# GpSimd's elementwise work in mixer and output projection on VectorE, and x scaled by both factors in one operation

## The chip, the cores and the metric

The kernel runs on one core of one Trainium2 chip. A core has TensorE (matrix products), VectorE (DVE in the rows), ScalarE (ACT), GpSimd (POOL) and SyncE (SP), which here issues every transfer between memory and the on-chip pages. Each engine takes its instructions in the order in which they were written, and waits at the first whose inputs aren't there. The metric is the device time of one execution in microseconds. The kernel before took 2190.82 us, the median of three runs (2187.02 to 2191.81).

## The reference

One layer of a streaming encoder on x of 512 tokens by 2048 features, all in fp32. The elementwise steps that this change touches are the norms, the recurrent group and the gated residual:

```python
mod = silu(c) @ w_ada + b_ada                       # six vectors: sh1, sc1, gt1, sh2, sc2, gt2
h = modulate(rms_norm(x, g_mix), sh1, sc1)          # rms_norm(x)*(1 + sc1) + sh1
xr, yr, q, k, v, f_logit = split(h @ w_in)
# recurrent group, per 128 channels
u = causal_depthwise_conv(xr, conv_w, conv_b)
r, i = sigmoid(u @ w_a + b_a), sigmoid(u @ w_x + b_x)
log_a = -8 * r * softplus(-lam)
b_in = sqrt(-expm1(2 * log_a)) * (i * u)
y_rec = scan(exp(log_a), b_in) * gelu(yr)
# attention group: per-head norms of q and k, causal softmax with a forget bias
y_att = forgetting_attention(q, k, v, f_logit)
mix = concat(rms_norm(y_rec, g_out_rec), rms_norm(y_att, g_out_att))
x = x + gt1 * (mix @ w_out)
h2 = modulate(rms_norm(x, g_ffn), sh2, sc2)
gate, up = split(h2 @ w_up)
x = x + gt2 * ((silu(gate) * up) @ w_down)
```

## The kernel before, in words

Pages hold 128 features by 512 tokens. Every matrix product is made of three fp32r products: each operand is split into a high and a low part, the high part a rounded copy by ScalarE, the low part the difference by VectorE. These splits of the streamed weights are the *wsplits* (L187 ScalarE, L188 VectorE); TensorE waits for both halves. Low parts of activations are VectorE's too: `hpl` (L334), `hl` (L374).

The program is written stage by stage, and a scheduler fixes each engine's order when the program is built, by priorities and by its own estimates. Nothing is chosen at run time.

- *w1 stage* (about 5 to 109 us, loop `for kt in range(KT)`, L321). For each block of 128 features VectorE makes the row sums of `w_ada` times silu(c) for sc1 (two operations of 1024 columns, `ada` and `adf`, L149), forms the factor `A`, and the low parts of x·A and of the weights; ScalarE makes the high parts and the square of x; GpSimd adds the square to `ssq_x` (L280); TensorE multiplies for the recurrent input xr. The norm's factor comes last: after the sixteen blocks `rstd_x` is formed from `ssq_x` (`rms_rstd` on GpSimd, `rstd_parts`).
- *h stage* (109 to about 203 us). TensorE makes the first half of yr (`yr0p`) and head 0's q, k and v (`h0p`). `make_h` (L364) makes the normalised input: x·A was already made in place by ScalarE (L370, run in the w1 stage), GpSimd multiplies by `rstd_x` (L371), ScalarE adds `sh1` and rounds (`hh`, L373), VectorE makes `hl`. `ada_fast` makes sh1 from another two operations `ada` and `adf` a block, and `sh` (L366).
- *Heads* (203 to 606 us). For h = 1 to 7 TensorE runs a group `h1p` to `h7p` of 192 matmuls, and between them the attention of the head before (`stats`, `qk_t`, `score`, `pt_`, `pv`). VectorE evacuates each group: for head 0 also the forget logits `z` (L416) and the copies `qk` (L451). In the first two heads the 48 pieces of the projection's bias are summed: `bias_in` loads a piece `bw` (L566, two buffers) and VectorE adds it to `ba` (L569, L571); `bias_sum` gives them to TensorE as `binp` (L576). With the bias there, four pairs of recurrent blocks run beside heads 3 to 7 (`rec_pair`): `conv` reloads xr and multiplies by `rstd_x` (L588, GpSimd), `gates` multiplies i by u (L618, GpSimd), `scan` by the square root (L628, GpSimd) and scans (L630, VectorE), `finish` makes the gelu (`gelu2`, L543 on GpSimd) and the sum of squares.
- *Output projection* (606 to about 795 us). Four groups of 192 matmuls (`wo0p` to `wo3p`). For the first three ScalarE copies the result out of PSUM and GpSimd multiplies by `st_att[0]` (L803, L804); `x1_fin` then adds x and the squares to `ssq_1`.
- *FFN* (from 795 us on): up projection in seven products of halves (`uf`), down projection (`dn`). The change does not touch it.

## Time and profile before

| | |
|---|---|
| median of three runs | 2190.82 us (2187.02, 2190.82, 2191.81) |
| the profiled execution | 2185.2 us, its span 2183.5 us |
| TensorE (PE) busy | 2114.4 us, 97% of the span |
| VectorE (DVE) busy | 1560.4 us, 71%, 2319 instructions |
| ScalarE (ACT) busy | 873.1 us, 40% |
| GpSimd (POOL) busy | 187.3 us, 9%, 129 instructions |
| transfers | 406.01 MB, mean 186 GB/s |

Shares over the whole span hide the stages. In the page's forty slices of 54.6 us TensorE is at nine tenths or more from the 23rd slice to the last, while VectorE is at eight or nine tenths in the first four. GpSimd works in the first fourteen slices only. The rows below are therefore read for stretches of the span. Times in them are microseconds from the span's start; a row of a group of instructions gives its number, the busy time, the mean in nanoseconds of one, and the idle time just before it with what ended it.

### The profile page before, as it was taken

Reading aid. Unit: us, or ns where it says so; the run is one execution under the profiler, and the core shown is the slowest. Engines: PE = TensorE matmul, PEld = TensorE weight load, DVE = VectorE, ACT = ScalarE, POOL = GpSimd, SP = SyncE. Lnnn points to the kernel's source line nnn. Section 1 sums busy time; section 2 is a strip of 40 time slices with the busy share of each in tenths; the row PEclk is TensorE's granted clock in tenths of the full one; section 3 lists DMA queues with packets and bytes.
Section 4 is the critical chain, followed back from the end, with each engine's and each line's share of the span. In section 5 each row is a group of like instructions: output and inputs, shape, how many; then the busy total and the mean of one; then the engine's idle time right before and its main releaser. Section 6 shows DMA issues by size and latency. Waiting matters only on the chain.

```text
span 2183.5 us, 32375 instructions
## 1 busy us (share of the span) xinstructions
PE 2114.4 (97%) x12737; PEld 1911.2 (88%) x12737; DVE 1560.4 (71%) x2319; ACT 873.1 (40%) x1224; POOL 187.3 (9%) x129
## 2 busy tenths in 40 slices
PE   8988989899989999999999999999999999999999
PEld 6777988788878888899999999999999888888887
DVE  8998668886687879988888888888888343322332
ACT  5523436665343335544444444444444222221111
POOL 2260012332012400000000000000000000000000
PEclk9999989999999999999999999999999999999999
DMA  9868666566667752343434444343444984553442
GB/s 320 319 209 301 220 217 212 197 211 236 215 228 259 252 193 97 129 133 126 145 118 131 139 131 131 126 141 121 128 143 149 338 312 174 189 197 134 155 156 103
DMA packets 133017, 406.01 MB, mean 186 GB/s; under 512 B 14561, under 2 KB 19841, under 8 KB 123138
## 3 DMA queue, kind: packets, MB, share of 16 engines
q1 hardware_dynamic: 132866, 403.96, 54.6%
q8 instruction: 99, 1.62, 0.3%
q14 instruction: 52, 0.43, 0.1%
HBM read 361.15 MB, written 42.75 MB: 185 GB/s over the span
## 4 chain that ended last, share of the span: by engine, by line
PE 77%; DVE 12%; DMA 6%; issue 3%; ACT 2%; POOL 1%; SPq 0%; DVEq 0%; POOLq 0%; ACTq 0%
PE dn_0p L192 5%; PE dn_3p L192 5%; PE dn_2p L192 5%; PE dn_1p L192 5%; PE up0p L192 2%; PE wo3p L192 2%; PE wo2p L192 2%; PE wo1p L192 2%; DVE adf L149 2%; PE wo0p L192 2%; DMA ada<-in_adaT 2%; PE yr1p L192 1%; PE h3p L192 1%; DMA bw<-in_wyr 1%; DVE ada L149 1%
## 5 line engine op out<-in xcount | busy, mean ns | idle before, releaser
L139 DVE SCALAR_TENSOR_TENSOR ada<-ada,c_b 128x1024 f32<-128x1024 f32 x128 | 163.7, 1296 | 34.1 <-DMA ada<-in_adaT 33.9
L188 DVE TENSOR_TENSOR uq_0tl<-uq_0r,uq_0th 128x1024 fp32r<-128x1024 f32 x40 | 49.0, 1225 | 61.8 <-ACT uq_0th L187 61.7
L187 ACT ACTIVATE uq_0sh<-uq_0r 128x1024 fp32r<-128x1024 f32 x40 | 42.5, 1062 | 90.6 <-PE uf33p L957 2.3
L188 DVE TENSOR_TENSOR uq_0al<-uq_0r,uq_0ah 128x1024 fp32r<-128x1024 f32 x40 | 49.0, 1225 | 39.1 <-ACT uq_0ah L187 39.1
L187 ACT ACTIVATE uq_1th<-uq_1ra 128x1024 fp32r<-128x1024 f32 x40 | 42.5, 1062 | 70.6 <-DVE uq_1sl L188 1.8
L187 ACT ACTIVATE uq_0th<-uq_0r 128x1024 fp32r<-128x1024 f32 x40 | 42.4, 1060 | 70.6 <-DVE uq_0r L937 1.9
L187 ACT ACTIVATE uq_1sh<-uq_1rb 128x1024 fp32r<-128x1024 f32 x40 | 42.5, 1062 | 70.3 <-PE uf43p L957 2.4
L187 ACT ACTIVATE uq_1ah<-uq_1ra 128x1024 fp32r<-128x1024 f32 x40 | 42.5, 1062 | 60.6 <-issue 59.1
L187 ACT ACTIVATE uq_0ah<-uq_0r 128x1024 fp32r<-128x1024 f32 x40 | 42.4, 1060 | 49.3 <-issue 46.8
L149 DVE SCALAR_TENSOR_TENSOR adf<-adf,c_b 128x1024 f32<-128x1024 f32 x32 | 56.4, 1763 | 1.7 <-DMA adf<-in_adaT 1.7
L188 DVE TENSOR_TENSOR uq_1tl<-uq_1ra,uq_1th 128x1024 fp32r<-128x1024 f32 x40 | 49.0, 1226 | 10.3 <-ACT uq_1th L187 10.2
L192 PE MATMUL w1p<-hph,w1h 128*128 128x512 f32 x128 | 48.7, 407 | 6.4 <-ACT hph L333 6.1
L192 PE MATMUL w1p<-hpl,w1h 128*128 128x512 f32 x128 | 51.8, 405 | 2.0 <-DVE hpl L334 1.9
L188 DVE TENSOR_TENSOR uq_0sl<-uq_0r,uq_0sh 128x1024 fp32r<-128x1024 f32 x40 | 49.1, 1226 | 3.6
L571 DVE SCALAR_TENSOR_TENSOR ba<-bw,sh,ba 128x512 f32<-128x512 f32 x45 | 34.2, 769 | 23.8 <-DMA bw<-in_w 12.5
L188 DVE TENSOR_TENSOR uq_1sl<-uq_1rb,uq_1sh 128x1024 fp32r<-128x1024 f32 x40 | 49.0, 1226 | 2.7 <-ACT uq_1sh L187 0.6
L192 PE MATMUL w1p<-hph,w1l 128*128 128x512 f32 x128 | 50.7, 396 | 0.0
L188 DVE TENSOR_TENSOR uq_1al<-uq_1ra,uq_1ah 128x1024 fp32r<-128x1024 f32 x40 | 48.7, 1216 | 0.1
L149 DVE SCALAR_TENSOR_TENSOR ada<-ada,c_b 128x1024 f32<-128x1024 f32 x32 | 41.2, 1288 | 2.6 <-DMA ada<-in_adaT 2.6
L188 DVE TENSOR_TENSOR dn_1l<-dn_2r,dn_1h 128x1024 fp32r<-128x1024 f32 x11 | 13.5, 1226 | 38.0 <-ACT dn_1h L187 38.0
L188 DVE TENSOR_TENSOR dn_0l<-dn_2r,dn_0h 128x1024 fp32r<-128x1024 f32 x11 | 13.5, 1225 | 37.6 <-ACT dn_0h L187 37.6
L188 DVE TENSOR_TENSOR dn_1l<-dn_0r,dn_1h 128x1024 fp32r<-128x1024 f32 x11 | 13.5, 1225 | 37.4 <-ACT dn_1h L187 37.4
(13791 smaller groups left out, 8322.5 us busy)
## 6 DMA issues: line engine op xcount, KB each, us to landing
ada<-in_adaT SPq DMA_DIRECT2D x160, 512.0 KB, 5.0
uq_0r<-in_wups SPq DMA_DIRECT2D x80, 512.0 KB, 4.2
uq_1ra<-in_wups SPq DMA_DIRECT2D x40, 512.0 KB, 4.0
uq_1rb<-in_wups SPq DMA_DIRECT2D x40, 512.0 KB, 3.2
adf<-in_adaT SPq DMA_DIRECT2D x32, 512.0 KB, 5.4
actd<-ach SPq DMA_DIRECT2D x44, 256.0 KB, 2.0
actd<-acl SPq DMA_DIRECT2D x44, 256.0 KB, 4.1
dn_0r<-in_wdown SPq DMA_DIRECT2D x11, 1024.0 KB, 4.9
```

The costliest lines, as they stand in the source:

```text
L139: nc.vector.scalar_tensor_tensor(out=t, in0=t, scalar=1.0, in1=cs, op0=ALU.mult, op1=ALU.mult, accum_out=ac)
L149: nc.vector.scalar_tensor_tensor(out=t, in0=t, scalar=1.0, in1=c_b[:, cs], op0=ALU.mult, op1=ALU.mult, accum_out=ada_acc[j][:, hf, i:i + 1])
L187: nc.scalar.activation(R(hi[:, :n]), raw_ap, AF.Copy)
L188: tail_lo.append(nc.vector.tensor_sub(R(lo[:, :n]), raw_ap, hi[:, :n]).ins)
L192: nc.tensor.matmul(ps, lhsT=R(l), rhs=R(r), start=start, stop=stop)
L571: nc.vector.scalar_tensor_tensor(out=ba[j], in0=src, scalar=s1, in1=ba[j], op0=ALU.mult, op1=ALU.add)
```

## The change

Nine places are edited. In the w1 stage, in attention, in the recurrent blocks and behind the output projection the sums of squares go from GpSimd to VectorE (`square_acc`). In `make_h` ScalarE's product by `A` and GpSimd's by `rstd_x` become one VectorE operation with both factors, which stands where the h stage needs it. The products of xr by `rstd_x`, of i by u and by the square root go to VectorE. Gelu's square goes from GpSimd to ScalarE. The result of the output projection is multiplied by `st_att[0]` by VectorE straight out of PSUM, without ScalarE's copy. GpSimd keeps the small operations of `rms_rstd` and the constants.

```diff
--- before.py
+++ after.py
@@ -271,13 +271,13 @@
         sums()
         return spread()
 
-    def square_acc(ssq, src, first, name, tag, eng=None):
+    def square_acc(ssq, src, first, name, tag):
         if first:
             nc.scalar.activation(ssq, src, AF.Square)
         else:
             sq = page(name, tag)
             nc.scalar.activation(sq, src, AF.Square)
-            (eng or nc.gpsimd).tensor_add(ssq, ssq, sq)
+            nc.vector.tensor_add(ssq, ssq, sq)
 
     def log1p_exp(dst, z, w, name):
         e = small(w, name + "e", 2)
@@ -367,8 +367,7 @@
                                        in1=vcol(V_BADA + SH1 * KT, kt), op0=ALU.add, op1=ALU.add)
         sh1.append(s1)
         t = xs[kt]
-        nc.scalar.activation(t, t, AF.Copy, scale=A[kt])
-        nc.gpsimd.tensor_mul(t, t, rstd_x)
+        nc.vector.scalar_tensor_tensor(out=t, in0=t, scalar=A[kt], in1=rstd_x, op0=ALU.mult, op1=ALU.mult)
         h, l = page(f"hh{kt}", "h"), page(f"hl{kt}", "h")
         nc.scalar.activation(R(h), t, AF.Identity, bias=s1)
         nc.vector.scalar_tensor_tensor(out=R(l), in0=t, scalar=s1, in1=h, op0=ALU.add, op1=ALU.subtract)
@@ -540,7 +539,7 @@
     hs = [None] * NB
     def gelu2(y, name, tag):
         w = page(name, tag)
-        nc.gpsimd.tensor_mul(w, y, y)
+        nc.scalar.activation(w, y, AF.Square)
         nc.vector.scalar_tensor_tensor(out=w, in0=w, scalar=1.0 / GELU_C, in1=y, op0=ALU.add, op1=ALU.mult)
         nc.scalar.activation(w, w, AF.Tanh, scale=GELU_C * GELU_S)
         nc.vector.scalar_tensor_tensor(out=w, in0=w, scalar=1.0, in1=y, op0=ALU.add, op1=ALU.mult)
@@ -585,7 +584,7 @@
             x = page(f"xrl{n}", "c")
             nc.sync.dma_start(out=x, in_=xr[n])
             X[n] = x
-            nc.gpsimd.tensor_mul(x, x, rstd_x)
+            nc.vector.tensor_mul(x, x, rstd_x)
             nc.scalar.activation(x, x, AF.Identity, bias=bin_[:, n:n + 1])
             u = page(f"u{n}", "c")
             nc.scalar.activation(u, x, AF.Identity, scale=vcol(V_CW, n * 4 + 3), bias=vcol(V_CB, n))
@@ -615,7 +614,7 @@
                 for n in ns:
                     last["exp"] = nc.scalar.activation(RG[n], RG[n], AF.Exp, scale=spn[:, n:n + 1])
             for n in ns:
-                nc.gpsimd.tensor_mul(IG[n], IG[n], U[n])
+                nc.vector.tensor_mul(IG[n], IG[n], U[n])
             for n in ns:
                 nc.vector.tensor_mul(U[n], RG[n], RG[n])
                 nc.vector.scalar_tensor_tensor(out=X[n], in0=U[n], scalar=1.0, in1=X[n], op0=ALU.add, op1=ALU.mult)
@@ -625,7 +624,7 @@
                 for n in ns:
                     nc.scalar.activation(X[n], X[n], AF.Sqrt, scale=-1.0)
             for n in ns:
-                nc.gpsimd.tensor_mul(IG[n], IG[n], X[n])
+                nc.vector.tensor_mul(IG[n], IG[n], X[n])
             for n in ns:
                 nc.vector.tensor_tensor_scan(out=U[n], data0=RG[n], data1=IG[n], initial=0.0, op0=ALU.mult, op1=ALU.add)
                 hs[n] = U[n]
@@ -651,7 +650,7 @@
     def rec_out(n, g):
         y = hs[n]
         nc.vector.scalar_tensor_tensor(out=y, in0=g, scalar=0.5, in1=y, op0=ALU.mult, op1=ALU.mult)
-        square_acc(ssq_rec, y, n == 0, f"sqr{n}", "c", nc.vector if n >= 4 else nc.gpsimd)
+        square_acc(ssq_rec, y, n == 0, f"sqr{n}", "c")
         if n < 4:
             hs[n] = drp.tile([P, S], F32, name=f"yrecd{n}")
             nc.sync.dma_start(out=hs[n], in_=y)
@@ -800,8 +799,7 @@
             t = page(f"x1_{kt}", "c")
             gt = mods[GT1][:, kt:kt + 1]
             if g < 3:
-                nc.scalar.activation(t, ps[f], AF.Copy)
-                nc.gpsimd.tensor_mul(t, t, st_att[0])
+                nc.vector.tensor_mul(t, ps[f], st_att[0])
             else:
                 xt = load_x(kt, "x3_")
                 nc.vector.scalar_tensor_tensor(out=t, in0=ps[f], scalar=gt, in1=st_att[0], op0=ALU.mult, op1=ALU.mult)
@@ -810,7 +808,7 @@
             if g < 3:
                 late.append(lambda t=t, kt=kt: x1_fin(t, kt))
             else:
-                square_acc(ssq_1, t, kt == 0, f"sq1_{kt}", "d", nc.vector)
+                square_acc(ssq_1, t, kt == 0, f"sq1_{kt}", "d")
             if g == 3:
                 with_a2()
             if g == 3 and f == 0:
```

The scheduler builds new orders from this. On VectorE in a block of the w1 stage (`adf`: the second product with `w_ada`; `A`: the factor; `w1l`: a weight's low part), the difference of the two orders:

```order
 L149 SCALAR_TENSOR_TENSOR adf_3_293,ada_acc_114<-adf_3_293,c_b 128x1024
 L328 SCALAR_TENSOR_TENSOR A_302<-ada_acc_114,bg 128x1
+L280 TENSOR_TENSOR ssq_x<-ssq_x,sqx_315 128x512
 L330 TENSOR_TENSOR A_302<-A_302,vec 128x1
 L341 TENSOR_TENSOR w1l_310<-w1r_0_298,w1h_309 128x512
```

The sum of squares stands between the two steps of `A`, in every block from the second on.

On VectorE at the end of the h stage, around the last `hl` and up to the first `z` of head 0 (`ba`: the sums of bias pieces `bw`; `h_0l`, `h_1l`: wsplits), before:

```order
L569 TENSOR_SCALAR ba_1810<-bw_1_1815,sh_0_1042 128x512
L569 TENSOR_SCALAR ba_1811<-bw_2_1818,sh_0_1042 128x512
L188 TENSOR_TENSOR h_1l<-h0r_1678,h_1h 128x784
L374 SCALAR_TENSOR_TENSOR hl_1663<-x_920,sh_15_1658,hh_1662 128x512
L571 SCALAR_TENSOR_TENSOR ba_1809<-bw_0_1849,sh_1_1068,ba_1809 128x512
L188 TENSOR_TENSOR h_0l<-h1r_1791,h_0h 128x768
L571 SCALAR_TENSOR_TENSOR ba_1810<-bw_1_1852,sh_1_1068,ba_1810 128x512
L571 SCALAR_TENSOR_TENSOR ba_1811<-bw_2_1855,sh_1_1068,ba_1811 128x512
L188 TENSOR_TENSOR h_1l<-h1r_1791,h_1h 128x768
L571 SCALAR_TENSOR_TENSOR ba_1809<-bw_0_1929,sh_2_1110,ba_1809 128x512
L416 TENSOR_TENSOR z<-h0p_1416,bfb 128x8
```

and in the same place now:

```order
L370 SCALAR_TENSOR_TENSOR x_920<-x_920,A_926,rstd_x 128x512
L188 TENSOR_TENSOR h_1l<-h1r_1775,h_1h 128x768
L366 SCALAR_TENSOR_TENSOR sh_15_1643<-ada_acc_113,vec 128x1
L568 TENSOR_SCALAR ba_1793<-bw_0_1796,sh_0_1042 128x512
L568 TENSOR_SCALAR ba_1794<-bw_1_1799,sh_0_1042 128x512
L373 SCALAR_TENSOR_TENSOR hl_1647<-x_920,sh_15_1643,hh_1646 128x512
L450 COPY qk_1720<-h0p_1407 128x256
L415 TENSOR_TENSOR z<-h0p_1406,bfb 128x8
```

Before, there are seven `ba` operations ahead of `z`, one above these rows and six in them. Now there are two; the others have gone behind `z`. The new last scaling of x (L370) stands in front of the last `sh`. The transfers of the two remaining pieces now stand beside those of blocks 6 and 7 of sh1.

On TensorE in head 2's stretch (`h3p`: the group of head 3; `binp`: the bias sums), the first `binp` with its neighbours before:

```order
L192 MATMUL h3p_2677<-h_0h,hl_1073 128x384
L192 MATMUL h3p_2678<-h_0h,hh_1072 128x384
L192 MATMUL h3p_2678<-h_0l,hh_1072 128x384
L192 MATMUL h3p_2678<-h_0h,hl_1073 128x384
L576 MATMUL binp<-ones,ba_1809 128x1 x4
L192 MATMUL h3p_2675<-h_1h,hh_1114 128x384
```

and now:

```order
L192 MATMUL h3p_2662<-h_0l,hh_1226 128x384
L192 MATMUL h3p_2662<-h_0h,hl_1227 128x384
L192 MATMUL h3p_2659<-h_1h,hh_1251 128x384
L192 MATMUL h3p_2659<-h_1l,hh_1251 128x384
L575 MATMUL binp<-ones,ba_1793 128x1 x4
L192 MATMUL h3p_2659<-h_1h,hl_1252 128x384
```

Before, 24 matmuls of h3 stand ahead of the first `binp`, now 74; what is ahead of h3 is the same. The matmuls of attention and gates keep their places.

## Rows read from the trace of the kernel before

**Rows 1.** Stretches: PE, PEld, DVE, ACT, POOL busy; PEclk, DMA share, GB/s.

```profile
20.00:104.00 84.00, 80.97 (x336) 61.30 (x335) 80.82 (x129) 43.15 (x71) 20.97 (x14) 1.00 0.93 327
...
117.00:149.00 32.00, 29.47 (x130) 24.07 (x129) 29.54 (x24) 7.58 (x10) 31.34 (x16) 1.00 0.47 163
149.00:200.00 51.00, 44.75 (x223) 40.81 (x222) 46.15 (x82) 16.50 (x22) 0.00 (x0) 0.97 0.84 286
...
314.00:555.00 241.00, 221.30 (x1143) 201.29 (x1144) 187.42 (x305) 147.27 (x258) 63.01 (x42) 0.95 0.63 211
...
664.00:840.00 176.00, 176.00 (x788) 146.06 (x787) 138.69 (x170) 66.47 (x89) 40.25 (x24) 1.00 0.65 221
```

**Rows 2.** Waits of PE over the span: us in total, times, longest.

```profile
PE s L495 <- DVE nm L499: 10.3, 4, 3.1
PE pt L509 <- DVE bt L503: 8.2, 5, 2.4
...
PE h1p L192 <- DVE z L416: 5.9, 1, 5.9
...
PE binp L576 <- DVE ba L571: 1.3, 1, 1.3
```

**Rows 3.** Timeline, one block of the w1 stage: start us, us, engine, line.

```profile
44.09 1.22 DVE L149 SCALAR_TENSOR_TENSOR ada<-ada,c_b 128x1024 f32<-128x1024 f32 x1
...
45.00 1.47 POOL L280 TENSOR_TENSOR ssq_x<-ssq_x,sqx 128x512 f32<-128x512 f32 x1 [4.51 <-ACT sqx L279]
...
45.23 2.31 DVE L149 SCALAR_TENSOR_TENSOR adf<-adf,c_b 128x1024 f32<-128x1024 f32 x1
...
49.46 0.69 DVE L341 TENSOR_TENSOR w1l<-w1r,w1h 128x512 fp32r<-128x512 f32 x1
...
50.07 1.22 DVE L149 SCALAR_TENSOR_TENSOR ada<-ada,c_b 128x1024 f32<-128x1024 f32 x1
```

**Rows 4.** Groups of instructions of DVE in 20:104.

```profile
L149 DVE SCALAR_TENSOR_TENSOR adf<-adf,c_b 128x1024 f32<-128x1024 f32 x14 | 31.2, 2229 | 0.0
```

**Rows 5.** Chain that ended last, in order of time: start us, us.

```profile
209.05 6.66 PE h1p L192 x24
...
229.35 4.17 PE h1p L192 x24
...
663.84 43.52 PE wo1p L192 x192
```

**Rows 6.** Timeline of POOL in 95:170.

```profile
117.34 31.34 POOL L371 TENSOR_TENSOR x<-x,rstd_x 128x512 f32<-128x512 f32 x16 [1.93 <-ACT rstd_x L265]
```

**Rows 7.** Groups of instructions of DVE in 117:150.

```profile
L149 DVE SCALAR_TENSOR_TENSOR adf<-adf,c_b 128x1024 f32<-128x1024 f32 x4 | 8.1, 2034 | 0.0
L374 DVE SCALAR_TENSOR_TENSOR hl<-x,sh,hh 128x512 fp32r<-128x512 f32 x5 | 8.1, 1621 | 3.5 <-ACT hh L373 3.5
L149 DVE SCALAR_TENSOR_TENSOR ada<-ada,c_b 128x1024 f32<-128x1024 f32 x4 | 7.0, 1761 | 0.0
L366 DVE SCALAR_TENSOR_TENSOR sh<-ada_acc,vec 128x1 f32<-128x1 f32 x3 | 3.6, 1190 | 0.0
```

**Rows 8.** Timeline of DVE: the last hl, the first z, the last ba.

```profile
198.59 0.74 DVE L374 SCALAR_TENSOR_TENSOR hl<-x,sh,hh 128x512 fp32r<-128x512 f32 x1
...
208.84 0.16 DVE L416 TENSOR_TENSOR z<-h0p,bfb 128x8 f32<-128x8 f32 x1
...
310.55 1.41 DVE L571 SCALAR_TENSOR_TENSOR ba<-bw,sh,ba 128x512 f32<-128x512 f32 x2
```

**Rows 9.** Groups of instructions of DVE in 314:606.

```profile
L468 DVE TENSOR_TENSOR qk<-qk,ss 128x512 f32<-128x512 f32 x10 | 14.1, 1445 | 9.1 <-POOL ss L241 9.1
```

**Rows 10.** One line's instructions: ns min/median/max, first and last start.

```profile
L630 DVE TENSOR_TENSOR_SCAN u<-g,g x8: 1192/2268/2303, 368.4 to 524.8; 128x512 f32<-128x512 f32 x8
```

**Rows 11.** Groups of instructions of POOL over the span.

```profile
L588 POOL TENSOR_TENSOR xrl<-xrl,rstd_x 128x512 f32<-128x512 f32 x8 | 13.8, 1728 | 29.8 <-DMA xrl<-xrd 28.8 <-issue 0.9
...
L628 POOL TENSOR_TENSOR g<-g,xrl 128x512 f32<-128x512 f32 x8 | 12.2, 1550 | 21.8 <-ACT xrl L626 21.8
```

## The prediction

> **What bounds the kernel now.** I read the table of stretches first [rows 1]. In 664–840 us TensorE is busy all the time, and the page shows the same for nearly everything behind it, so whatever the change does there is hidden. The gaps lie in the first 664 us: 3.0 us in 20–104, 2.5 in 117–149, 6.3 in 149–200, 19.7 in 314–555. Up to 200 us VectorE is the fullest engine (80.8 of 84, 29.5 of 32, 46.2 of 51 us), while the transfers take 0.93, 0.47 and 0.84 of their engines' time. TensorE's own waits [rows 2] name VectorE most: the scores and the transposes of the weights in attention, and one wait of 5.9 us for `z`. So the question is whether VectorE, which receives 88 more operations of 512 columns, becomes fuller or emptier.
>
> **Term 1, the w1 stage (20–104 us).** One block of 128 rows shows it [rows 3]. GpSimd's sum starts at 45.00 and holds until 46.47. The `adf` product that VectorE starts at 45.23 takes 2.31 us, its twin `ada` of the same shape 1.22: it ends 1.1 us after GpSimd does. This is no accident of one block: all fourteen `adf` here average 2229 ns [rows 4]. So each GpSimd sum costs VectorE 1.09 us. On VectorE the sum costs 0.61 (a `w1l` of its shape starts at 49.46, the next instruction at 50.07). Net −0.48 of a block that lasts 5.98 us (`ada` at 44.09 and 50.07); 14 blocks, −6.7. Two floors lie close. TensorE needs 24 matmuls of 0.227 us (192 in 43.52 [rows 5]), 5.44 a block, which would allow −7.5. The transfers at full share would take 0.93 of 5.98, 5.56, which allows −5.9. Since all three then lie within 0.15 us of each other, I take −5.5, bounds −1 (transfers slow down near their limit) and −7.
>
> The Trainium skill's page "Perfetto Trace Analysis", section "Optimizing Scalar/DVE Operations", points the other way: where VectorE is saturated, hand work to ScalarE or even GpSimd; it adds that the two share a read port, so that it might not help. By the advice alone this stage would become 14 x 0.61 = 8.5 us longer; by its second sentence, and by [rows 3], it becomes shorter. The skill's page "SBUF — State Buffer", section "Who interferes with whom", calls that port pair an exclusive lock, on which the second to start waits for the whole of the first; the end of this `adf`, 1.1 us behind GpSimd's, agrees.
>
> **Term 2, the h stage (104–200 us).** GpSimd does all sixteen products x·rstd in one piece, 31.3 us from 117.34 on [rows 6]. VectorE's operations in that time are long [rows 7]: four `adf` at 2.03 and four `ada` at 1.76 for 1.22, five `hl` at 1.62 for 0.74 [rows 8], three `sh` of one column at 1.19, for which I count 0.22: 3.3 + 2.2 + 4.4 + 2.9 = 12.8 us of blocking, and by the same 1.09 two more wsplits, some 15 in all. After the change VectorE scales x itself, sixteen operations with two page operands and one column scalar. That is the form of `hl`: 0.74 us, less the 0.08 by which an instruction here overlaps the next (`w1l` lasts 0.69, the next starts after 0.61), 0.66; bounds 0.61 and 0.74. 16 x 0.66 = 10.6: net −4.4. At the stage's head some 0.7 more goes, since a GpSimd product stood between `rstd_x` and the first `hh`, and VectorE's short waits for transfers late in the stage should shrink, as its demand is now even. Against that the spills of xr move into this stage, and TensorE comes within 2 us of being the bound. I take −5, bounds 0 and −9.
>
> **Term 3, the hand-over to head 0 (200–209 us).** The last `hl` ends at 199.33, but the evacuation `z` runs only at 208.84 [rows 8]: VectorE, which takes instructions in order, stands before `ba` sums whose weights are still in transfer. TensorE waits 5.9 us for it [rows 2], and its first 24 matmuls after that take 6.66 us, against 4.17 for 24 later ones [rows 5]. In the new order (shown with the change) seven `ba` operations ahead of `z` have become two, with weights that were asked for some thirty transfers earlier. So `z` should follow the last `hl` by some 3 us instead of 9.5: −6.5, and up to −2.5 from the slow matmuls. I take −8, bounds −4 and −9.
>
> **Term 4, what is late next.** Those five operations aren't gone. After `z`, 46 `ba` operations with a load each remain in place of 41. Before, 41 took from 208.84 to 311.96 [rows 8], 2.5 us each, through two buffers. TensorE's `binp` needs the last of them and waited 1.3 us for it [rows 2], so the two paths were even. In the new order the first `binp` stands 50 matmuls of h3 later, 8.7 us at 0.174 (24 in 4.17 [rows 5]). TensorE now reaches it 8.7 − 1.3 − 2.5 (the slow matmuls) = 4.9 us later after `z` than before, other waits unchanged. Five more loads at 2.5 us are 12.5 us: a wait of some 8, up to 12 where the other waits shorten. With two buffers the loads can also go faster (two of 3.6 us at a time are 1.8 each), and then nothing waits. I take +5, bounds 0 and +12.
>
> **Term 5, the recurrent pairs (314–606 us).** 32 products and sums move: 32 x 0.61 = 19.5 us more on VectorE. What it gets back stands in its long operations: 10 `qk` at 1445 ns [rows 9] for the 0.69 of a `w1l`, 7.6 us; 8 scans, half of them over 2268 ns where the shortest took 1192 [rows 10], some 6; smaller ones I put at 8. Its waits for GpSimd's products before the scans go as well, and partly become waits for ScalarE's roots. So VectorE is about as full as before or some us emptier, and each product ends 0.7 to 1 us sooner. TensorE's waits for VectorE in the attention are 18.5 us [rows 2]; I let a quarter go: −4, bounds −12 and +9 (both below). Gelu's square goes to ScalarE, four times 0.6 us (estimate, by VectorE's 0.61), on an engine that is idle for 94 of 241 us [rows 1].
>
> **Term 6, output projection.** Twelve products go from GpSimd, behind a ScalarE copy, to one VectorE operation out of PSUM, and eleven sums of squares follow. TensorE has no gap in 664–840; its cover is VectorE's 37 idle us there (176 − 138.7 [rows 1]), while 23 x 0.61 = 14 come on. 0; without cover at most +14, which I don't count.
>
> Sum: −5.5 − 5 − 8 + 5 − 4 = −17.5 us. The profiled execution took 2185.2 us (span 2183.5 and 1.7 around it), so 2167.7; the median of the timed runs is 5.6 above it, 2190.8. Against that median I predict 2173 us, with 2164 to 2183 as its own range: the bounds of the terms seldom fall on one side together.
>
> **Rivals.**
> *More.* If TensorE's waits in attention are mostly the work of blocked VectorE operations, term 5 is −12, and with term 4 at 0 the sum is −30.5: 2160. For it: the two long groups of waits [rows 2] are for VectorE. Against: VectorE's queue there stays nearly as long as it was.
> *The transfers bind.* The first stage stands at 0.93 already [rows 1]. If that is the ceiling, terms 1 and 2 shrink to −1 each, and the loads of term 4, closer together, cost +8; with −8 and −2 the sum is −4: 2187. Against: 117–149 ran at 0.47, so there is room to bring loads forward.
> *Slower: waits at the head of VectorE's queue.* GpSimd stood idle 28.8 us for the reloads of xr and 21.8 for ScalarE's roots [rows 11] with nobody behind it; on VectorE the wsplits that feed TensorE stand behind these products. If half of the 50 us lands there and half of that reaches TensorE, term 5 is −4 + 13 = +9; with term 3 at −4 and term 4 at +12 the sum is +6.5: 2197. It decides from some 20 us of new VectorE idle time on. Against: much of this idle time is GpSimd being early, and the new order puts the products behind other work.
> *Slower: a full VectorE only gets fuller.* Were no blocking given back, terms 1 and 2 would be +8.5 and +10.6; with −8 and +5, +16: 2207. [Rows 3 and 7] speak against it. This is what the advice of "Perfetto Trace Analysis" in the Trainium skill would lead one to expect.
>
> **How the numbers follow.** Forecast 0.62, more 0.16, transfers 0.11, queue 0.08, fuller 0.03. A difference below 0.2% (4.4 us) can't be told from none here. Slower: the last two, less 0.01 for a mild queue, 0.10. Same: half of the transfers' case and 0.02 of the forecast's tail, 0.08. Faster: the rest, 0.82. The range for eight in ten runs from the larger gain, 2160, to just past the transfers' case, 2188.
>
> **What would show it.** Term 1: `adf` at 1.22 us throughout, a block of 5.4 to 5.6 us. Term 2: no `hl` above 0.8 us, the last `hl` 8 to 13 us before 199.3. Term 3: no wait of TensorE for `z` above 2 us, h1's first matmul near 190. Term 4: a wait before `binp` of some 5 us. Term 5: scans at 1.2 us, less of TensorE's time lost before scores, no VectorE idle time above 3 us before the products with xr. Behind 915 us all is shifted and nothing else. I am wrong if a block stays near 6 us, or if h4 to h7 take longer than before.

## The result and the profile after

The changed kernel takes 2161.57 us (median of four runs, 2160.31 to 2162.5), the kernel before beside it 2191.32 (four runs, 2187.02 to 2192.39): ratio 0.9868, 95% interval 0.9852 to 0.9883, or 29 us less. The forecast was 2173 with a range of 2160 to 2188, so the sign was right and the time lies near the range's lower end, outside the likeliest case's own 2164 to 2183. The profiled execution took 2160.95 us (before: 2185.2). The profiles are thus 24 us apart where the medians are 30: the profiled run of the kernel before is one of its faster ones, and leads over its profile come out some 5 us small by the end of the span.

First the same stretches as in [rows 1], the columns are as there:

```profile
20.00:104.00 84.00, 84.00 (x376) 69.35 (x374) 80.30 (x158) 37.76 (x63) 0.00 (x0) 1.00 0.96 350
117.00:149.00 32.00, 32.00 (x143) 26.50 (x142) 32.00 (x55) 10.19 (x14) 0.00 (x0) 1.00 0.92 315
149.00:200.00 51.00, 49.26 (x277) 48.31 (x275) 46.49 (x93) 17.45 (x29) 1.84 (x2) 1.00 0.88 303
314.00:555.00 241.00, 221.09 (x1158) 197.58 (x1157) 187.21 (x340) 150.93 (x265) 13.77 (x10) 0.98 0.65 218
664.00:840.00 176.00, 176.00 (x790) 146.12 (x789) 135.31 (x201) 66.62 (x88) 2.17 (x2) 1.00 0.58 198
```

In 20–104 us TensorE has no gap left and does 376 matmuls where it did 336; VectorE, as full as before, does 158 operations for 129. The transfers go at 350 GB/s, so 327 was not their ceiling. TensorE's waits over the span, which answer to [rows 2]:

```profile
PE pt L508 <- DVE bt L502: 14.3, 8, 4.0
PE s L494 <- DVE nm L498: 10.5, 5, 3.1
...
PE binp L575 <- DVE ba L570: 3.8, 1, 3.8
...
PE pc L422 <- DVE lf L420: 3.0, 1, 3.0
...
PE h3p L192 <- ACT v L453: 2.5, 1, 2.5
```

The wait for `z` is gone, that for `binp` has grown from 1.3, that of `pc` for `lf` from 0.2; `h3p` waited for `v` before too (3.1). The two of attention are longer in sum than before (24.8 us for 18.5). One block of the w1 stage, VectorE, in order of time, answers to [rows 3]:

```profile
43.02 1.22 DVE L149 SCALAR_TENSOR_TENSOR adf<-adf,c_b 128x1024 f32<-128x1024 f32 x1
...
44.42 0.69 DVE L280 TENSOR_TENSOR ssq_x<-ssq_x,sqx 128x512 f32<-128x512 f32 x1
...
48.38 1.22 DVE L149 SCALAR_TENSOR_TENSOR adf<-adf,c_b 128x1024 f32<-128x1024 f32 x1
```

A block lasts 5.36 us (43.02 to 48.38), and `adf` is short. Groups of VectorE in 101–185 us, the h stage (for [rows 7]):

```profile
L149 DVE SCALAR_TENSOR_TENSOR adf<-adf,c_b 128x1024 f32<-128x1024 f32 x15 | 18.2, 1215 | 0.0
L370 DVE SCALAR_TENSOR_TENSOR x<-x,A,rstd_x 128x512 f32<-128x512 f32 x16 | 11.9, 744 | 2.8 <-ACT rstd_x L265 2.8
L373 DVE SCALAR_TENSOR_TENSOR hl<-x,sh,hh 128x512 fp32r<-128x512 f32 x16 | 11.9, 744 | 0.0
```

The scaling costs 0.744 us each, as `hl` does, and nothing is held up. The last `hl` and the first `z` (for [rows 8]), and the bias sums over the span with their idle time:

```profile
182.05 0.75 DVE L373 SCALAR_TENSOR_TENSOR hl<-x,sh,hh 128x512 fp32r<-128x512 f32 x1
...
184.04 0.17 DVE L415 TENSOR_TENSOR z<-h0p,bfb 128x8 f32<-128x8 f32 x1
```

```profile
L570 DVE SCALAR_TENSOR_TENSOR ba<-bw,sh,ba 128x512 f32<-128x512 f32 x45 | 33.3, 749 | 27.7 <-DMA bw<-in_w 14.7 <-DMA bw<-in_wyr 13.0
```

Before, the last of these rows was

```profile
L571 DVE SCALAR_TENSOR_TENSOR ba<-bw,sh,ba 128x512 f32<-128x512 f32 x45 | 34.2, 769 | 23.8 <-DMA bw<-in_w 12.5 <-DMA bw<-in_wyr 11.1
```

`z` follows the last `hl` by 1.2 us where it followed by 9.5. VectorE waits 27.7 us for bias weights; it waited 23.8 us for them before, so the wait itself is hardly new, only its place is. Groups of VectorE in 314–606 us, for [rows 9 to 11]:

```profile
L629 DVE TENSOR_TENSOR_SCAN u<-g,g 128x512 f32<-128x512 f32 x8 | 9.5, 1213 | 0.0
L467 DVE TENSOR_TENSOR qk<-qk,ss 128x512 f32<-128x512 f32 x10 | 6.5, 688 | 9.0 <-POOL ss L241 9.0
L627 DVE TENSOR_TENSOR g<-g,xrl 128x512 f32<-128x512 f32 x8 | 5.5, 686 | 0.3
...
L587 DVE TENSOR_TENSOR xrl<-xrl,rstd_x 128x512 f32<-128x512 f32 x7 | 4.8, 688 | 4.8 <-DMA xrl<-xrd 4.8
```

Every operation is now about as short as the shortest of its kind before (1192 ns for a scan, 0.69 us for a `w1l`). GpSimd's idle time before these products (28.8 and 21.8 us) has become 4.8 and 0.3 us of VectorE's.

To see where the 24 us of the two profiles are, I split the span at the first matmul of each group. A stretch is given as its length, what TensorE idled in it, and (1 − granted clock) x length, both worked out from the rows of the stretches; the last is what the stretch lost by being granted 0.50, the lower of the two levels (1.2 GHz for 2.4), for a part of it. The clock has two decimals in the rows, so this last figure is good to about 1 us in the long stretches.

| us | before | after |
|---|---|---|
| w1 (from 20) | 89.3 / 3.4 / 0 | 81.4 / 0 / 0 |
| yr0 and h0 | 99.8 / 16.4 / 2.6 | 83.0 / 2.7 / 0 |
| h1 to h3 | 140.3 / 7.2 / 9.3 | 151.1 / 17.2 / 8.9 |
| h4 to h7 | 205.1 / 19.7 / 10.3 | 199.6 / 18.7 / 6.0 |
| yr1 | 51.6 / 0.6 / 0 | 51.9 / 0 / 0 |
| wo0 | 57.6 / 5.8 / 3.5 | 52.4 / 4.5 / 0 |

7.9 us come from w1, 16.8 from yr0 and h0, 10.8 are lost again in h1 to h3, and 5.5 and 5.2 come from h4–h7 and wo0. Behind wo0 all is shifted by 24.2 to 24.6 us and nothing else.

### The profile page after: what moved, and what is told of

The parts are those of the page before. It is cut to its first block, busy times and chain, and to the rows that moved or that the text cites. A ratio compares the mean times of both kernels' runs of the same rounds, so it can differ in the third digit from the quotient of the medians.

```text
span 2158.9 us, 32248 instructions
## 1 busy us (share of the span) xinstructions
PE 2099.0 (97%) x12737; PEld 1904.1 (88%) x12737; DVE 1532.5 (71%) x2407; ACT 859.0 (40%) x1200; POOL 32.9 (2%) x37
## 4 chain that ended last, share of the span: by engine, by line
PE 82%; DVE 8%; DMA 6%; issue 2%; ACT 1%; POOL 1%; SPq 0%; DVEq 0%; ACTq 0%
PE dn_0p L192 6%; PE dn_3p L192 6%; PE dn_2p L192 6%; PE dn_1p L192 6%; PE w1p L192 4%; PE yr1p L192 2%; PE up0p L192 2%; PE wo3p L192 2%; PE wo2p L192 2%; PE wo1p L192 2%; PE up1p L192 2%; PE yr0p L192 2%; DMA bw<-in_w 2%; DMA ada<-in_adaT 2%; PE wo0p L192 2%
## 5 line engine op out<-in xcount | busy, mean ns | idle before, releaser
L139 DVE SCALAR_TENSOR_TENSOR ada<-ada,c_b 128x1024 f32<-128x1024 f32 x128 | 154.7, 1219 | 50.0 <-DMA ada<-in_adaT 49.9
L570 DVE SCALAR_TENSOR_TENSOR ba<-bw,sh,ba 128x512 f32<-128x512 f32 x45 | 33.3, 749 | 27.7 <-DMA bw<-in_w 14.7
L149 DVE SCALAR_TENSOR_TENSOR ada<-ada,c_b 128x1024 f32<-128x1024 f32 x32 | 38.9, 1217 | 2.4 <-DMA ada<-in_adaT 2.4
L188 DVE TENSOR_TENSOR dn_0l<-dn_0r,dn_0h 128x1024 fp32r<-128x1024 f32 x11 | 13.5, 1226 | 37.0 <-ACT dn_0h L187 37.0
```

Of the source, the lines that this page charges most:

```text
L139: nc.vector.scalar_tensor_tensor(out=t, in0=t, scalar=1.0, in1=cs, op0=ALU.mult, op1=ALU.mult, accum_out=ac)
L149: nc.vector.scalar_tensor_tensor(out=t, in0=t, scalar=1.0, in1=c_b[:, cs], op0=ALU.mult, op1=ALU.mult, accum_out=ada_acc[j][:, hf, i:i + 1])
L188: tail_lo.append(nc.vector.tensor_sub(R(lo[:, :n]), raw_ap, hi[:, :n]).ins)
L570: nc.vector.scalar_tensor_tensor(out=ba[j], in0=src, scalar=s1, in1=ba[j], op0=ALU.mult, op1=ALU.add)
```

## The experiments

Each kernel was timed against the kernel before, on the same chip. The last column is the difference of the two ratios to before, times 2190 us; since the intervals are about ±0.0015 to 0.002, it is good to some 5 us.

| kernel | median us | ratio to before, 95% interval | against the changed kernel |
|---|---|---|---|
| changed | 2161.57 | 0.9868 [0.9852, 0.9883] | |
| e1: w1 sums back on GpSimd | 2165.93 | 0.9898 [0.9878, 0.9917] | +7 |
| e2: scaling of x back | 2165.54 | 0.9898 [0.9880, 0.9916] | +7 |
| e3: unread GpSimd sums added | 2173.88 | 0.9935 [0.9919, 0.9952] | +15 |
| e4: wide loads of bias weights | 2143.23 | 0.9796 [0.9775, 0.9816] | −16 |
| e5: all of the pairs' operations back | 2180.95 | 0.9963 [0.9948, 0.9977] | +21 |
| e6: output projection back | 2159.34 | 0.9866 [0.9848, 0.9884] | 0 |
| e7: before, wide loads | 2181.95 | 0.9964 [0.9952, 0.9976] | +21 |
| e8: before, scaling alone | 2184.43 | 0.9979 [0.9965, 0.9993] | +24 |
| e9: pairs' products back | 2173.57 | 0.9932 [0.9920, 0.9945] | +14 |
| e10: pairs' sums and squares back | 2159.65 | 0.9869 [0.9855, 0.9883] | 0 |
| e11: wide loads, pairs back | 2153.89 | 0.9856 [0.9836, 0.9876] | −3 |
| e12: before, pairs alone | 2172.05 | 0.9925 [0.9909, 0.9941] | +12 |

**e1, the sums of the w1 stage.**

```
-        square_acc(ssq_x, xt, kt == 0, f"sqx{kt}", "c")
+        square_acc(ssq_x, xt, kt == 0, f"sqx{kt}", "c", nc.gpsimd)
```

> The changed kernel (2161.6 us) with only the fifteen sums of squares of x, in the w1 stage, back on GpSimd. Port theory (a GpSimd operation holds a running two-operand VectorE product up until it ends): adf back at 2.2 to 2.3 us from 1.22, a block back from 5.4 to 6.0 us, yr0's first matmul some 8 us later (109 instead of 101.4) and the whole some 8 us later, 2169 to 2170. Rival, that the stage is now bound by TensorE and the transfers and would be so with the sums on GpSimd too: no block above 5.5 us, 2161 to 2163. Second rival, that the later stages are bound by their loads, which run on while the w1 stage is slow: the block is back at 6.0 but half of it is made up by h1, 2165.

The long product is back, VectorE's groups in 20–109 us:

```profile
L149 DVE SCALAR_TENSOR_TENSOR ada<-ada,c_b 128x1024 f32<-128x1024 f32 x15 | 32.6, 2174 | 0.0
...
L149 DVE SCALAR_TENSOR_TENSOR adf<-adf,c_b 128x1024 f32<-128x1024 f32 x15 | 18.2, 1216 | 0.0
```

This time it is `ada` that lies beside GpSimd's sum; the price is the same, 0.96 us each. yr0's first matmul is at 110.2 instead of 101.4. The timed difference, 7 us by the ratios and 4 by the medians (2165.93, where the second rival had 2165), is near the theory's 8. The two intervals just overlap; the trace's 8.8 us and e3 carry the verdict. The second rival, that h1 makes up half, doesn't hold: the lag is 8.7 us at h1 and still 9.1 at the end of wo0.

**e3, the same sums for nobody.** VectorE keeps its work; GpSimd adds x into a page that nothing reads.

```
+    scr = cp.tile([P, S], F32, name="scr", tag="ssq", bufs=2)
+    nc.gpsimd.memset(scr, 0.0)
...
         square_acc(ssq_x, xt, kt == 0, f"sqx{kt}", "c")
+        if kt:
+            nc.gpsimd.tensor_add(scr, scr, xt)
```

> The changed kernel, and in each block of the w1 stage but the first one more sum of 512 columns on GpSimd, of x into a page that nobody reads; VectorE keeps all its own work. Port theory: VectorE's products that run beside it grow by about 1.1 us a block as adf did before; VectorE has some 5.1 us of work in a block of 5.4, so the block becomes 6.2 to 6.6 us and the whole 12 to 18 us slower, 2174 to 2180. Rival, that in the kernel before the wait for GpSimd's result (ssq, the page sqx coming free) and not its presence cost the time: no change, 2160 to 2163.

15 us slower, and no engine waits for the result of the added work. Fifteen blocks (360 matmuls) of the changed kernel:

```profile
20.00:101.00 81.00, 81.00 (x359) 66.90 (x358) 77.30 (x152) 35.31 (x60) 0.00 (x0) 1.00 0.96 350
```

and of e3:

```profile
20.00:116.00 96.00, 87.73 (x361) 66.10 (x360) 93.16 (x156) 34.83 (x60) 20.15 (x14) 1.00 0.86 296
```

The groups of e3 in that stretch, GpSimd's and two of VectorE's:

```profile
L346 POOL TENSOR_TENSOR scr<-scr,x 128x512 f32<-128x512 f32 x14 | 20.2, 1446 | 69.3 <-DMA x<-in_xT 69.3
...
L149 DVE SCALAR_TENSOR_TENSOR adf<-adf,c_b 128x1024 f32<-128x1024 f32 x15 | 19.4, 1293 | 0.0
...
L332 DVE TENSOR_TENSOR A<-A,vec 128x1 f32<-128x1 f32 x14 | 7.6, 543 | 0.0
```

14 sums of 1.45 us make VectorE's busy time 15.9 us longer and the fifteen blocks 15 us longer. Some 1.5 of the 15.9 are two more instructions that fall into the stretch; what is left is 1.03 us for each sum. I had expected the products to carry it; here it is spread over all that VectorE does, down to an operation of one column (543 ns; 152 in the changed kernel). The rival, a wait for GpSimd's result, has fallen. The Trainium skill's page "SBUF — State Buffer", section "Who interferes with whom", calls the port pair that the two engines share an exclusive lock. 1.03 us of the 1.45 for each added sum agrees with a lock better than with an even sharing of the time, which would be half; no run here shows the ports themselves.

**e2 and e8, the scaling of x.** e2 undoes it in the changed kernel, e8 does it alone in the kernel before (the same lines the other way).

```
-        nc.vector.scalar_tensor_tensor(out=t, in0=t, scalar=A[kt], in1=rstd_x, op0=ALU.mult, op1=ALU.mult)
+        nc.scalar.activation(t, t, AF.Copy, scale=A[kt])
+        nc.gpsimd.tensor_mul(t, t, rstd_x)
```

> The changed kernel with only the scaling of x in the h stage as it was (ScalarE times A, GpSimd times rstd_x). This also brings back the order around z (eleven sums and z as in the kernel before) and binp's place in h3. Theory (terms 2, 3 and 4 are all this edit, -8.6, -8.2 and +10.8 by first matmuls): the last hl 8 to 9 us later, a wait of TensorE of some 6 us for z, and a lead at h4 as large as at h1: together 4 to 8 us slower than the changed kernel, 2166 to 2170. Rival, that the loss behind h1 (13.9 of lead left at h4 from 24.7) comes from VectorE's added work in the recurrent pairs and not from the moved bias sums: the lead still falls by some 10 us between h1 and h4, and the whole is 15 to 18 us slower, 2177 to 2179.

> The kernel before the change with only the scaling of x in the h stage as one VectorE operation. Theory (terms 2 to 4 all belong to this edit and add up with the others): the last hl 8 to 9 us earlier, h1's first matmul 16 to 17 us earlier, a lead of 4 to 8 us left at h4 and at the end, 2183 to 2187. Rival, that the first bias sums' loads get through only because the w1 stage before them is shorter: h1's lead is under 10 us and nothing is left at h4, 2189 to 2193. Second rival, that h1's loss comes with the recurrent pairs' operations on VectorE: the lead of 16 us stays to the end, 2173 to 2176.

The last `hl` and the first `z` of e2:

```profile
190.57 0.74 DVE L374 SCALAR_TENSOR_TENSOR hl<-x,sh,hh 128x512 fp32r<-128x512 f32 x1
...
201.00 0.16 DVE L416 TENSOR_TENSOR z<-h0p,bfb 128x8 f32<-128x8 f32 x1
```

and of e8:

```profile
190.49 0.75 DVE L373 SCALAR_TENSOR_TENSOR hl<-x,sh,hh 128x512 fp32r<-128x512 f32 x1
...
192.49 0.17 DVE L415 TENSOR_TENSOR z<-h0p,bfb 128x8 f32<-128x8 f32 x1
```

Undone, the last `hl` comes 8.5 us later and `z` another 8.4 us; done alone, 8.1 and 8.2 us earlier. So terms 2 and 3 both belong to this edit, 8 us each. And so does the loss: e2 leads the kernel before by 7.9 us at h1 and still by 8.0 at h4, while e8 leads by 16.3 at h1 and by 0.4 at h4. What is left of the edit is 7 us (e2) or 4.6 (e8), within the 4 to 8 that were expected of both; by its median e2 is only 4 us slower. The rival, that the pairs' operations cause the loss, has fallen: in e8 they are on GpSimd and it is all lost.

**e4 and e7, the bias weights.** e4 loads them wide in the changed kernel, e7 in the kernel before.

(Only the new lines; they replace three loads of 512 columns each.)

```
+        bw = ap_.tile([P, 1024], F32, tag="ada", name=f"bw{kt}")
+        nc.sync.dma_start(out=bw, in_=w1[kt])
+        bw2 = ap_.tile([P, S], F32, tag="x", name=f"bw{kt}_2", bufs=2)
+        nc.sync.dma_start(out=bw2, in_=wyr[0][kt // 4][:, (kt % 4) * 512:(kt % 4 + 1) * 512])
+        for j, src in enumerate((bw[:, :512], bw[:, 512:], bw2)):
```

> The changed kernel with the w1 pieces of the bias sums loaded 1024 columns at a time into the two pages of the ada blocks, which are idle then; only the wyr piece stays in the two pages of 512 columns. Theory (the loss of 10.8 us of lead between h1 and h4 is the chain of loads through two small pages): the wait before binp goes to under 1 us, the lead at h4 is 20 us or more instead of 13.9, and the whole is 4 to 8 us faster than the changed kernel, 2154 to 2158. Rival, that the loads are bound by the transfers' rate: lead and time as in the changed kernel, 2160 to 2163. Second rival, that the first bias sums stand ahead of z with their weights in transfer again: z waits for them 2 to 4 us, and the whole is within 3 us of the changed kernel.

> The kernel before the change (2191 us) with only the wide loads of the bias weights; all of GpSimd's work stays on GpSimd. Theory (the chain of loads through two small pages paces h1 to h3 in the kernel before too, though TensorE's wait for binp is only 1.3 us): h1 to h4 last some 130 us instead of 140.3, z is waited for 2 to 4 us less, and the whole is 9 to 14 us faster, 2177 to 2182; the change is then still worth 24 us or more where the loads don't hold it back (2143 against it). Rival, that only the changed kernel's order makes these loads late: within 2 us of before, 2189 to 2193, and the change is then worth 45 us with wide loads.

16 us faster, twice what I expected, and the fastest kernel here. Its bias sums over the span:

```profile
L571 DVE SCALAR_TENSOR_TENSOR ba<-bw,sh,ba 128x512 f32<-128x512 f32 x45 | 32.5, 744 | 3.8 <-DMA bw<-in_wyr 2.0 <-DMA bw<-in_w 1.8
```

The wait of 27.7 us is 3.8, and h1 to h3 last 132.7 us (idle 3.6) instead of 151.1. So the transfers had room, and the chain of 48 loads through two small pages was what held. The edit gives two more pages and also makes 32 loads of 48, half of them twice as wide; these runs don't say which of the two it takes. In the kernel before the same edit is worth 8 us, a little under what I expected. The difference, some 8 us, is what the changed order costs by these loads; with wide loads on both sides the change is worth 0.9796 to 0.9964, some 37 us instead of 29.

**e5, e9, e10, e11 and e12, the recurrent pairs.** e9 has the three products, e10 the rest, e5 both; e11 is e5 on top of e4; e12 is e5 the other way round, in the kernel before.

```
-            nc.vector.tensor_mul(x, x, rstd_x)
+            nc.gpsimd.tensor_mul(x, x, rstd_x)
...
-                nc.vector.tensor_mul(IG[n], IG[n], U[n])
+                nc.gpsimd.tensor_mul(IG[n], IG[n], U[n])
...
-                nc.vector.tensor_mul(IG[n], IG[n], X[n])
+                nc.gpsimd.tensor_mul(IG[n], IG[n], X[n])
```

```
-        nc.scalar.activation(w, y, AF.Square)
+        nc.gpsimd.tensor_mul(w, y, y)
...
-                square_acc(ssq_att, y, h == 0, f"sqa{h}", "b")
+                square_acc(ssq_att, y, h == 0, f"sqa{h}", "b", nc.gpsimd)
...
-        square_acc(ssq_rec, y, n == 0, f"sqr{n}", "c")
+        square_acc(ssq_rec, y, n == 0, f"sqr{n}", "c", nc.vector if n >= 4 else nc.gpsimd)
```

> The changed kernel with all of term 5 back on GpSimd: the products with rstd_x, with U and with the roots in the recurrent pairs, gelu's square, the sums of squares of heads and of the first four recurrent rows. Theory (scans and products on VectorE run beside GpSimd's and are held up): scans back at 2.2 to 2.3 us, h4's first matmul as in the changed kernel (335.5), wo0's 5 to 7 us later (592 to 594), the whole 5 to 8 us slower, 2166 to 2169 where the changed kernel has 2161. Rival, that the lead of the pairs is only the place at which the stages happen to meet: wo0 within 2 us of 587 and 2160 to 2163. Second rival, that VectorE's queue got longer by these operations: faster by 2 to 6 us, 2155 to 2159.

> The changed kernel with only the 24 products of the recurrent pairs (with rstd_x, U and the roots) back on GpSimd; gelu's square and the sums of squares stay as changed. Undoing both together cost some 20 us (2181 against 2161). Theory (what costs is the long hold-ups: scans at 2.2 us beside the second products, and VectorE waiting for the products before each scan): 60 to 70% of it, 2172 to 2176, scans at 2.2 to 2.3 us, the products of q and k with ss short at 0.7. Rival, that it is the sums, which fall on the products with ss and on the head of the output projection: within 3 us of the changed kernel, 2158 to 2164.

> The changed kernel with only gelu's square and the sums of squares of heads and of the first four recurrent rows back on GpSimd; the 24 products stay on VectorE. Theory: 30 to 40% of the 20 us, 2166 to 2170, with the products with ss back at 1.4 us, scans at 1.2, and wo0 at 55 us or more. Rival, that these fourteen operations cost nothing because GpSimd holds nobody up who is late: 2159 to 2163. Second rival, that they cost all of it: 2178 or more.

> The kernel with wide loads of the bias weights (2143 us), and the pairs' products, squares and sums back on GpSimd. Theory (of the 20 us that this cost with small pages, 7 came by way of the bias sums between h1 and h4, 13 are the pairs' own): 2155 to 2161, the lead at h4 within 2 us of the wide kernel's. Rival, that nearly all of the 20 us was the bias sums' chain meeting a longer VectorE queue: 2145 to 2149. Second rival, that the pairs' own share is larger when nothing else holds TensorE up: 2162 to 2166.

> The kernel before the change (2191 us) with only the pairs' part of it (24 products, four squares, ten sums off GpSimd); the order around z, and the w1 and h stages, stay as before. Theory (the pairs' operations are worth 10 to 20 us by themselves): h4's first matmul within 2 us of 349.4, the lead grows from there on, 2172 to 2181. Rival, that they pay only with the new order at z: within 4 us of before, 2187 to 2193. Second rival, that alone they lengthen VectorE's queue and cost: 2195 or more.

e5 costs 21 us, three times what I expected, the products by themselves 14 (e9, as expected), the sums and squares by themselves nothing (e10, against my expectation, though the rival had named it). With wide loads the pairs are worth 13 us (e11), alone in the kernel before 16 (e12), as the theories had it (e11's 2153.89 lies 1 us below the range given for it). So this is the largest part of the change. Groups of e5 in 314–606 us, VectorE's scans and products with `ss`:

```profile
L629 DVE TENSOR_TENSOR_SCAN u<-g,g 128x512 f32<-128x512 f32 x8 | 14.7, 1882 | 4.7 <-POOL g L627 4.7
...
L467 DVE TENSOR_TENSOR qk<-qk,ss 128x512 f32<-128x512 f32 x10 | 14.1, 1447 | 9.1 <-POOL ss L241 9.1
```

They are as long as before the change. Over the span, the same two groups of e9 and then of e10:

```profile
L629 DVE TENSOR_TENSOR_SCAN u<-g,g 128x512 f32<-128x512 f32 x8 | 14.7, 1881 | 4.7 <-POOL g L627 4.7
...
L467 DVE TENSOR_TENSOR qk<-qk,ss 128x512 f32<-128x512 f32 x16 | 19.0, 1230 | 11.8 <-POOL ss L241 11.8
```

```profile
L629 DVE TENSOR_TENSOR_SCAN u<-g,g 128x512 f32<-128x512 f32 x8 | 9.4, 1211 | 0.0
...
L467 DVE TENSOR_TENSOR qk<-qk,ss 128x512 f32<-128x512 f32 x16 | 10.4, 689 | 13.5 <-POOL ss L241 13.5
```

Both of my expectations on the `ss` products were wrong: it is the 24 products of the pairs that make them long, not the sums. Where the 21 us arise, in length / idle / (1 − clock) x length:

| us | changed | e5 | e4 | e11 | e12 |
|---|---|---|---|---|---|
| h1 to h3 | 151.1 / 17.2 / 8.9 | 158.1 / 23.7 / 8.3 | 132.7 / 3.6 / 5.2 | 132.2 / 5.8 / 1.9 | 139.7 / 8.5 / 6.4 |
| h4 to h7 | 199.6 / 18.7 / 6.0 | 207.6 / 19.4 / 14.5 | 195.0 / 14.6 / 5.9 | 201.4 / 20.0 / 6.0 | 199.8 / 17.1 / 6.0 |
| wo0 | 52.4 / 4.5 / 0 | 57.3 / 6.0 / 3.4 | 54.8 / 5.4 / 1.6 | 56.1 / 4.7 / 3.4 | 56.6 / 5.1 / 3.4 |

e5 against the changed kernel: 7 us in h1 to h3, 8 in h4 to h7, 5 in wo0. In h4 to h7 of these two profiles TensorE idles about as long; what differs is how often it is then slow. h4 to h7 of the changed kernel, and of e5:

```profile
335.50:535.10 199.60, 180.94 (x954) 162.76 (x954) 157.78 (x286) 131.82 (x229) 11.03 (x8) 0.97 0.64 214
```

```profile
342.50:550.10 207.60, 188.16 (x956) 169.84 (x954) 163.57 (x257) 130.24 (x225) 59.12 (x41) 0.93 0.62 206
```

The same 955 matmuls take 188.2 us instead of 180.9. Read in pieces of 3 us, the granted clock falls to 0.50 five times in e5, twice in the changed kernel and four times in the kernel before. Two of e5's falls:

```profile
417.50:420.50 3.00, 0.56 (x4) 0.24 (x2) 3.00 (x4) 1.01 (x3) 0.04 (x1) 0.96 0.23 88
420.50:423.50 3.00, 2.50 (x8) 2.32 (x9) 3.00 (x3) 2.98 (x6) 1.50 (x1) 0.50 0.44 118
423.50:426.50 3.00, 3.00 (x11) 3.00 (x11) 3.00 (x7) 1.93 (x3) 0.00 (x0) 0.50 0.84 323
426.50:429.50 3.00, 3.00 (x13) 2.21 (x12) 3.00 (x12) 1.84 (x6) 0.03 (x1) 0.90 0.73 209
435.50:438.50 3.00, 0.00 (x0) 0.00 (x0) 2.79 (x6) 1.36 (x2) 0.17 (x1) 0.81 0.73 281
438.50:441.50 3.00, 2.84 (x11) 2.84 (x12) 1.57 (x3) 1.60 (x3) 0.56 (x1) 0.50 0.73 246
```

TensorE idles some 3 us (2.4 and 0.5, then 3.0), and its matmuls are slow for some 7 us after that (a piece at 0.90 counted as slow for a fifth of it). Every fall in h4 to h7 of the two kernels stands behind 2.7 to 5 us of idle time; several waits of 1 to 2 us had none behind them. The length of a wait doesn't settle it alone, though. The kernel before idles for 3.0 us and runs on at full clock:

```profile
376.40:379.40 3.00, 0.00 (x0) 0.00 (x0) 3.00 (x8) 1.05 (x2) 0.00 (x0) 1.00 1.02 406
379.40:382.40 3.00, 2.98 (x14) 2.51 (x15) 2.96 (x7) 2.25 (x6) 1.09 (x1) 1.00 0.67 231
```

So a wait costs itself, and a long one often, not always, about 3 us again (14.5 us over five falls in e5, 6.0 over two in the changed kernel). Against e4, e11 shows the pairs' cost in the same stretch the other way: idle 20.0 for 14.6 at the same clock loss. So a pair of profiles doesn't tell whether the cost reaches TensorE as idle time or as slow matmuls. All fourteen profiles together do, and h4 to h7 fall into two groups that don't overlap in length or idle time (range, then mean):

| h4 to h7, us | length | idle | (1 − clock) x length |
|---|---|---|---|
| products on VectorE: changed, e1, e2, e3, e4, e6, e10, e12 | 191.5 to 199.8, 197.1 | 12.2 to 18.7, 15.5 | 3.8 to 8.0, 5.9 |
| products on GpSimd: before, e5, e7, e8, e9, e11 | 201.4 to 207.6, 204.8 | 19.4 to 20.8, 20.0 | 6.0 to 14.5, 9.2 |

The products cost some 7.7 us in this stretch, 4.5 of them idle time and 3.3 slow matmuls. The 18.7 us of idle time in the changed kernel's profile are the most of its group.

How far VectorE is held up can be estimated from its busy time in h4 to h7. It is 163.7 us in e9 with 22 operations fewer than the changed kernel's 157.8, and 158.6 in e10 with 7 fewer; at 0.69 us for each that went, the others became some 21 and 6 us longer. The 21 cost the kernel 14 us, the 6 nothing that the timing shows. Not separated is the hold-up from the two other things that an edit here brings: each product takes 1.4 to 1.7 us on GpSimd for 0.69, and the scheduler writes another order. No run adds unread GpSimd work beside the pairs, as e3 does in the w1 stage, so that the hold-up is what costs there is argued, not shown.

The 7 us between h1 and h3 are not explained, but they recur: with the changed order at `z` and the small pages, h1 to h3 last 149.0 to 152.9 us in the five profiles with the products on VectorE (changed, e1, e3, e6, e10) and 156.2 to 158.1 in the three with them on GpSimd (e5, e8, e9). Only three of the pairs' operations on GpSimd lie there in e5, and its instructions stand in another order as well (one VectorE product of the pairs runs already in h1 in the changed kernel). With wide loads it vanishes (132.2 for 132.7), so it works by way of the bias loads. Nor do e9 and e10 add up to e5 (14 + 0 for 21), a gap about as large as the intervals allow.

**e6, the output projection.**

```
-                nc.vector.tensor_mul(t, ps[f], st_att[0])
+                nc.scalar.activation(t, ps[f], AF.Copy)
+                nc.gpsimd.tensor_mul(t, t, st_att[0])
...
-                square_acc(ssq_1, t, kt == 0, f"sq1_{kt}", "d")
+                square_acc(ssq_1, t, kt == 0, f"sq1_{kt}", "d", nc.gpsimd)
```

(The second stands in `x1_fin`, so it is for the first twelve rows. The last four stay on VectorE, as in the kernel before; the expectation's "all" says more than the edit does.)

> The changed kernel with only the output projection's part as before: a ScalarE copy and a GpSimd product for the first twelve rows, and all the sums of squares of x1 on GpSimd. Theory (term 6 is worth nothing; the 5 us that wo0 gained come from the stage's head, which this edit doesn't touch): wo0 lasts 52 to 55 us as in the changed kernel, 2160 to 2163. Rival, that the gain of wo0 is of these operations: wo0 lasts 57 to 58 us as in the kernel before, 2166 to 2167. Second rival, that the x1 sums at the end of the projection, on the way to the first weights behind it, now come late: up0 or up1 2 to 6 us longer.

The time stays, as expected, but not the lengths: h4 to h7 are 3.7 us shorter in this profile and wo0 is 59.2 us at a granted clock of 0.88, which the rival would have read as its loss; wo0 still ends where the changed kernel's does (639.6 and 639.4). The first GpSimd product of the projection starts at 638.4, about 1 us before wo0 ends, so these operations can't have made the rest of wo0 long, except by way of the new order. wo0 lasts 52.4 to 54.9 us in the changed kernel and in e1 to e4, where it has the changed kernel's code, and its idle time is 4.5 to 5.8 us in these and in e6; what differs is the clock. So wo0 in one profile is only good to some 3 us, and its gain is not shown to be term 6's.

## Why the prediction was right, and where it was not

- **Term 1 (−5.5).** Right in mechanism (e1, e3), a little small: 7.9 us by the first matmul of yr0, 7 by e1. I had put a block at 5.4 to 5.6 us; it takes 5.36 and TensorE is now the bound. I had held back for transfers at 0.93; they went to 0.96 and 350 GB/s.
- **Term 2 (−5).** The last `hl` is 16.5 us earlier, 7.9 of it term 1: −8.6, near the bound of −9, and more in all than the 8 to 13 us that I had named as its sign; e2 and e8 give 8.5 and 8.1. The blocking I had counted, some 15 us, all went; the discount for the spills of xr wasn't needed.
- **Term 3 (−8).** 8.3 us (9.5 to 1.2); e2 and e8 give 8.4 and 8.2. By the order of the instructions, as forecast.
- **Term 4 (+5).** The mechanism was right: the wait before `binp` is 3.8 us where some 5 were forecast, and wide loads remove it. The size is some 8 us by e4 less e7. The failing words are "other waits unchanged": the sums that wait for weights also stand ahead of the operations that feed TensorE in h1 to h3, whose idle time rose from 7.2 to 17.2 us, 2.5 of them at `binp`.
- **Term 5 (−4, bounds −12 and +9).** This is the step that failed, in size. Its VectorE side held: in h4 to h7 VectorE is busy 157.8 us with 286 operations where it was 163.2 with 257, and scans take 1.2 us. The step from there was "TensorE's waits for VectorE in the attention are 18.5 us; I let a quarter go". For the idle time that was about right: 4.5 us less in h4 to h7 over the fourteen profiles, though only 1.0 between those of before and after (18.7 for 19.7), and the two rows of waits that I had gone by even rose (24.8 us). But the pairs are worth 13 to 21 us (e5, e11, e12), outside the bounds. What the term put at nothing are the slow matmuls behind the waits, 3.3 us in h4 to h7 over the fourteen profiles (between before and after 4.3 of the 5.5 us there, and 3.5 of the 5.2 in wo0), and 5 to 7 us in h1 to h3, where few of these operations lie and the cause is open. I had priced slow matmuls behind a wait in terms 3 and 4 [rows 5] and left them out here. The rest of the 13 to 21 is not located.
- **Term 6 (0).** Right as far as the timing of e6 goes, to some 5 us.

Summed by undoing one part at a time the change is worth 7 + 7 + 21 + 0 = 35 us, against 29 measured together; the intervals allow this gap, so an overlap of the parts is not shown. The forecast came within 12 us because errors met: terms 1 and 2 were 6 us too small and term 5 some 9 or more, term 4 was 3 to 6 us off the other way. The sign and the mechanisms of terms 1 to 4 were right; that the time lies inside the range, 1.6 us from its lower end, is in part luck.

The rivals: "more" had the time (2160) and term 5's size, but with term 4 at 0, which is wrong. The transfers don't bind (e4). Waits at the head of VectorE's queue come to 5.1 us for xr and the roots, far from the 20 from which that case decides. "A full VectorE only gets fuller" left term 5 out of its sum, which by the same reasoning would have added 32 x 0.61, some 20 us. This rival, which the Trainium skill's page "Perfetto Trace Analysis", section "Optimizing Scalar/DVE Operations", would lead one to by its advice to hand work of a saturated VectorE to GpSimd, is the opposite of e1, e3 and e5. The page's own reservation, that handing work between these two might not help because they share a read port, agrees with them (15 us lost in e3).

## What to carry to other kernels

An operation on GpSimd beside a busy VectorE can be paid for by VectorE: look in the timeline for VectorE instructions that last longer than their twins, and count the excess before calling GpSimd's time free. Then ask who waits, since some 6 us of such excess cost nothing in e10. When a hand-over comes earlier, ask which loads were hidden ahead of it and through how many pages they go; here fewer and wider loads through two more pages gave half as much again as the whole change. And price a wait of TensorE with the slow matmuls behind it, by the granted clock of the stretch, from several profiles: the same code idled 14.6 us in h4 to h7 of one kernel and 18.7 in another.
